# RWKV mixer, heads 6 to 11: half of the matrices with exchanged chunk partitions, common units for all heads, a new order

## Chip, cores and metric

One core of a Trainium2 chip runs the whole kernel in one launch. The metric is the device time of one execution in microseconds (us); the time before is the median of three runs, 1074.89 us (1074.24 to 1075.43). The profile is of one execution more, 1075.53 us, whose span from first to last instruction is 1073.7 us.

## What is computed

A trunk of two layers on 256 tokens of width 1024, batch 1, all in float32. Each layer is a SwiGLU feed-forward (width 2816), a mixer with memory attention beside it, and a second SwiGLU, each followed by a layer norm. Layer 0's mixer is RWKV-7 with 12 heads of 64, layer 1's a stick-breaking attention.

```
for i in range(2):
    x = LN(ALPHA*x + 0.5*swiglu(x, ffn1[i]))
    p = x @ W_in[i]
    mix = rwkv7(p) if i == 0 else stick_breaking(p)
    h = concat(mix, memory_attention(p))
    x = LN(ALPHA*x + h @ w_out[i])
    x = LN(ALPHA*x + 0.5*swiglu(x, ffn2[i]))
# RWKV-7, for each head and token:
sa    = state @ kk_t
state = state*w_t - outer(sa, kk_t*a_t) + outer(v_t, k_t)
out_t = state @ r_t        # then a norm over the head, a bonus r.k.r_k * v, and a gate
```

## The kernel before

**Tiling.** The 256 tokens are two halves of 128, one token a partition. A feed-forward is 11 blocks of 256 columns. A block loads its gate, up and down weights (3 MB, six or more pieces of 128x1024), splits each piece into a high and a low part (`hi` on ScalarE, `lo` on VectorE; `piece`, line 638), and multiplies by three fp32r matmuls for each product (`mm3`, line 666). In a "whole" block the down weights stay plain f32 and take one f32 matmul instead. A block can be run for both halves on one load, or for one half ("solo", line 1503), so that one half's feed-forward can fill TensorE while the other half is in its mixer.

**The RWKV mixer** (`rwkv`, line 968) works on one half, which has two chunks of 64 tokens. A chunk's recurrence becomes triangular 64x64 matrices a head: `L` and its inverse (`T`, and its transpose `Tt`, built from 16x16 blocks by two rounds of products with `Lm` and `Y`), `Sk` and `RB` (decayed key and receptance products), `V`, and the turned `kn` and `bn`. In these tiles partitions 0 to 63 hold chunk 0 and partitions 64 to 127 chunk 1, for all 12 heads. Two heads share a state tile `S` by partitions. The last part is, chunk by chunk: X = Sk V (+ q S), U = -Tt X, S = S + kn V + bn U, output = Sk' V + r S + RB U.

Every one of these products is 64 rows by 64 columns. The partitions of its operands fix the row group of TensorE that it uses, the partitions of its result the column group. `product` (line 1233) multiplies six heads for both chunks, with operands and result on the same partitions; the loops of lines 1275 to 1339 do the rest.

**Order.** No instruction is issued as it is written: `Plan` (line 134) records all of them with an estimated cost, `order` (line 349) makes a list schedule for the five engines, and `improve` (line 545) repeats that `ROUNDS` times from a random seed and keeps the order that its own estimate finds shortest. Instructions in a `together` block (line 147) stay one unit on TensorE. `alternate` (line 1477) runs a mixer and feed-forward blocks of the other half side by side: each `yield` of the mixer adds the weight that the table `RW` has for its name, and for each 1.0 one step of filler follows. `LAGS`, `FIRST`, `HOLD` and `TAIL` say which blocks are solo and where they stand; `NRAW`, `NHI`, `NLO` are the buffers of weight pieces; `copy` (line 212) may go to ScalarE or VectorE. PSUM has two banks of each of four names: `gu`, `tp`, `acc0`, `acc1`.

Since all instructions are issued from line 602, the profile names groups by tiles: `T_339r`, `Y_340r` and so on are buffers, and later tiles in the same buffer carry the first one's name: X stands in `L_345r` (L), U and the transposed b in `Lm_330r`, V in `vn_311r`, kn in `kn_310r`, bn in `bn_384r`.

Of the kernel before, what the change touches and what calls it, by code (L numbers as in the profile page):

```python
# [21 lines left out]
P = 128  # L22
# [5 lines left out]
C = 64  # L28
# [35 lines left out]
MEMTAG = 'gu'  # L64
# [3 lines left out]
ORDERS = ((0, 1, 2, 3), (3, 0, 1, 2), (1, 0, 3, 2), (3, 0, 1, 2))  # L68
# [58 lines left out]
ROUNDS = 24  # L127
SHAKES = (0.0, 100.0, 300.0)
PATIENCE = 8
SEED = 8617  # L130
# [475 lines left out]
def kernel(ctx, tc, const, x, mem, f1g, f1u, f1d, f2g, f2u, f2d, ln_g, ln_b, w_out, w_mem_kv,  # L606
# [361 lines left out]
    def rwkv(hf, res):  # L968
# [54 lines left out]
        gate = sl("g")  # L1023
        for g in range(2):
            gp = ps(ac)
            nc.tensor.matmul(gp[:, :384], zl[:, 1], R["gup"][:, g * 384:(g + 1) * 384], start=True, stop=True)
            nc.copy(gate[:, g * 384:(g + 1) * 384], gp[:, :384])
# [73 lines left out]
        def nat(src, dst):  # L1101
            for j0, n in ((0, 4), (4, 2)):
                pt = ps("tp")
                with nc.together():
                    for i in range(n):
                        nc.tensor.transpose(pt[:, i * P:(i + 1) * P], src[:, j0 + i], ident)
                nc.copy(dst[:, j0 * P:(j0 + n) * P], pt[:, :n * P])

        hv = lambda t: t.rearrange("p (h d) -> p h d", d=HD)
        par = lambda t: t.rearrange("q (j p) d -> q j p d", p=2)  # L1110
        v = zv.rearrange("p j t -> p (j t)")
        nat(zv, v)
        V = hv(v)

# [10 lines left out]
        def narrow(a, b):  # L1125

            banks = [ps(next(tg))[:, :384].rearrange("q (j t) -> q j t", j=NT) for _ in range(2)]
            with nc.together():
                for j in range(NT):
                    for p, c in ((0, 0), (1, 1), (1, 0), (0, 1)):  # L1130
                        pr, cs = slice(p * HD, (p + 1) * HD), slice(c * C, (c + 1) * C)
                        nc.tensor.matmul(banks[p][cs, j], a(pr, j, cs), b(pr, j, cs), start=True, stop=True)
            yield from enumerate(banks)
# [54 lines left out]
        def put_back(x, scratch, dst):  # L1188
            nc.vector.transpose(scratch, x)
            sv = v4(scratch, True)[:, :, :, :NH]  # L1190
            for b in range(2):
                src = sv[:, :, b].rearrange("p s h -> p h s")
                nc.copy(dst[:, :, BLK * b:BLK * b + BLK], src, quad[:, 0:1])
                nc.copy(dst[:, :, 32 + BLK * b:32 + BLK * b + BLK], src, quad[:, 1:2])

        for p, sv in narrow(lambda *i: bt[i], lambda *i: qr[i[0], i[1], 1, i[2]]):
            nc.vector.tensor_tensor(par(RB)[:, :, p], sv, bc(mqr[:, 1], 1, [P, NT, C]), ALU.mult)
            yield "rb"
        for g in range(2):
            js = slice(3 * g, 3 * g + 3)  # L1200
            banks = [ps(next(tg))[:, :384].rearrange("q (i x t) -> q i x t", i=3, x=2) for _ in range(2)]
            with nc.together():
                for i in range(3):
                    for p, c in ((0, 0), (1, 1), (1, 0), (0, 1)):
                        pr, cs = slice(p * HD, (p + 1) * HD), slice(c * C, (c + 1) * C)
                        nc.tensor.matmul(banks[p][cs, i], kt[pr, 3 * g + i, cs], qr[pr, 3 * g + i, :, cs], start=True, stop=True)
# [9 lines left out]
        put_back(Xs[0], sl("Tt")[:, :512], T)  # L1216
        s2 = sl("Y")[:, :512]
        Tt = hv(sl("Tt"))
        put_back(Xs[1], s2, Tt)

        Lm = hv(sl("Lm"))
        for lastl in (False, True):
# [10 lines left out]
            def product(a, b, g, tag):  # L1233
                sv = ps(tag)[:, :384].rearrange("q (i t) -> q i t", i=6)
                with nc.together():
                    for i in range(6):
                        for c in range(2):
                            cs = slice(c * C, (c + 1) * C)
                            nc.tensor.matmul(sv[cs, i], a[cs, 6 * g + i], b[cs, 6 * g + i], start=True, stop=True)
                return sv  # L1240

            for g in range(2):
                gs = slice(6 * g, 6 * g + 6)
                tag = (ac, "tp")[g]
                y = product(Lm, Tt, g, tag)
                nc.copy(Y[:, gs], y)
                yield "dy"
            for g in range(2):
                gs = slice(6 * g, 6 * g + 6)
                tag = (ac, "tp")[g]  # L1250
                if not lastl:
                    tn = product(Y, T, g, tag)
                    yield "dt"
                ttn = product(T, Y, g, tag)
                yield "dt"
                if not lastl:
                    nc.vector.tensor_sub(T[:, gs], T[:, gs], tn)
                nc.vector.tensor_sub(Tt[:, gs], Tt[:, gs], ttn)

        hb = hv(sl("T"))  # L1260
        nc.vector.tensor_tensor(hb, V, bc(vm, 2, [P, NH, HD]), ALU.add)
        nc.vector.tensor_tensor(hb, hb, bc(bon, 2, [P, NH, HD]), ALU.mult)
# [3 lines left out]
        nc.vector.tensor_tensor(lb, lb, hv(gate), ALU.mult)  # L1266
        lg = hv(sl("T"))
        nc.sync.dma_start(lg, r_lng[0].partition_broadcast(P).rearrange("p (h d) -> p h d", d=HD))
        nc.vector.tensor_tensor(lg, lg, hv(gate), ALU.mult)

        X, U, o = hv(sl("L")), hv(sl("Lm")), hv(sl("Y"))
        six = lambda tag: [ps(tag)[:, :384].rearrange("q (i t) -> q i t", i=6) for _ in range(2)]
        both = [slice(c * C, (c + 1) * C) for c in range(2)]
        xb, Ov = six("tp"), six(ac)
        with nc.together():
            for i in range(NH):
                for cs in both:
                    nc.tensor.matmul(xb[i // 6][cs, i % 6], Sk[cs, i, 0], V[cs, i], start=i % 6 == 0, stop=i % 6 == 5)
        nc.copy(X[:, 0:6], xb[0])
        nc.copy(X[:, 6:12], xb[1])  # L1280
        yield "c0"
        own = []

        def from_pairs():
            with nc.together() as made:
                for i in range(NH):
                    for c, cs in enumerate(both):
                        nc.tensor.matmul(Ov[i % 2][cs, i // 2], Sk[cs, i, 1], V[cs, i], start=i < 2 and (hf == 0 or c == 1), stop=False)
            own.extend(made)

        if hf == 0:
            from_pairs()
        for c, cs in enumerate(both):
            first = hf == 0 and c == 0
            before = []
            if not first:
                with nc.together() as before:
                    for j in range(NT):
                        for p in range(2):
                            pr = slice(p * HD, (p + 1) * HD)  # L1300
                            nc.tensor.matmul(Ov[p][cs, j], qr[pr, j, 1, cs], S[pr, j], start=j == 0 and c == 0, stop=False)
                xs = six("tp")
                with nc.together() as made:
                    for j in range(NT):
                        for p in range(2):
                            pr = slice(p * HD, (p + 1) * HD)
                            nc.tensor.matmul(xs[p][cs, j], qr[pr, j, 0, cs], S[pr, j], start=True, stop=True)
                made[0].after.append(before[0].i)
# [3 lines left out]
            ub = six("tp")  # L1312
            with nc.together() as made:
                for i in range(NH):
                    nc.tensor.matmul(ub[i // 6][cs, i % 6], Tt[cs, i], X[cs, i], start=True, stop=True)
                    if c == 1:
                        nc.tensor.matmul(Ov[i % 2][both[0], i // 2], RB[both[0], i], U[both[0], i], start=False, stop=i >= NH - 2)
            solved = made[0].i
            if hf > 0 and c == 0:
                from_pairs()  # L1320
                own[0].after.append(solved)
            nc.copy(U[cs, 0:6], ub[0][cs], -1.0)
            nc.copy(U[cs, 6:12], ub[1][cs], -1.0)
            yield "c2"
            if not (hf == NHALF - 1 and c == 1):
                sb = ps("tp")[:, :MIX // 2].rearrange("q (j d) -> q j d", j=NT)
                for a, b in ((kn, V), (bn, U)):
                    with nc.together() as made:
                        for h in range(NH):
                            pr = slice(h % 2 * HD, (h % 2 + 1) * HD)  # L1330
                            nc.tensor.matmul(sb[pr, h // 2], a[cs, h * HD:(h + 1) * HD], b[cs, h],
                                             start=a is kn and h < 2, stop=a is bn and h >= NH - 2)
                made[0].after.append(own[0].i)
                nc.vector.tensor_tensor(S, S, sb, ALU.add)
                nc.vector.tensor_tensor(S, S, bc(pc[:, :, c], 2, [P, NT, HD]), ALU.mult)
                yield "c3"
        with nc.together():
            for i in range(NH):
# [234 lines left out]
```

## Time and profile before

| | us | share of the span |
|---|---|---|
| median of three runs | 1074.89 | |
| the profiled execution | 1075.53 | |
| its span | 1073.7 | |
| TensorE (PE) busy | 1055.9 | 98% |
| VectorE (DVE) busy | 880.6 | 82% |
| ScalarE (ACT) busy | 730.2 | 68% |
| weight queue, 302.12 MB | | 85% of 16 DMA engines |

PE is TensorE's matmuls, PEld its weight loads. Matmuls overlap: the length given for one is longer than the distance to the next, so the pace of a unit is read from starts. An f32 matmul leaves two records, an fp32r matmul one. "x24" is the number of records merged in a row. In the view of waits a row is: who waited <- for whom: total us, times, longest.

### The profile page before, as it was taken

The numbers are of one execution on the slowest core, as the hardware profiler recorded it, in microseconds if no ns is written. First come the engines' busy times: TensorE is split into PE (matmuls) and PEld (weight loads), VectorE is DVE, ScalarE is ACT, GpSimd is POOL, SyncE is SP. The second block draws the span as 40 slices with busy tenths as digits, with TensorE's granted clock in tenths as the row PEclk, the third lists the DMA queues.
The fourth block names the chain that finished last, engine by engine and source line by source line (L and its number), as shares of the span: only waits on it lengthen the run. The fifth ranks groups of instructions, "written<-read, shape, count | busy, mean of one in ns | idle before, by whom it ended". The sixth has DMA issues, their size and how long they took to land.

```text
span 1073.7 us, 17563 instructions
## 1 busy us (share of the span) xinstructions
PE 1055.9 (98%) x6253; PEld 848.2 (79%) x6253; DVE 880.6 (82%) x1227; ACT 730.2 (68%) x1037; POOL 4.3 (0%) x18
## 2 busy tenths in 40 slices
PE   7999999999999999999999999999999999999996
PEld 5888887877778777778888888888777777888885
DVE  5676669897999997886699865659799989998796
ACT  5665558865689784565577655538896999767672
POOL 0000000000000000000000000000000000000000
PEclk9999999999999999999999999999999999999999
DMA  9997869677888797698989976658988988999892
GB/s 292 334 364 250 255 207 357 203 241 240 257 292 290 243 303 252 204 345 293 296 290 365 342 231 205 216 174 293 366 268 293 366 294 281 371 367 347 292 328 90
DMA packets 212538, 303.24 MB, mean 282 GB/s; under 512 B 13876, under 2 KB 159456, under 8 KB 212450
## 3 DMA queue, kind: packets, MB, share of 16 engines
q1 hardware_dynamic: 212450, 302.12, 85.0%
q8 instruction: 49, 0.80, 0.3%
q14 instruction: 39, 0.32, 0.1%
HBM read 301.01 MB, written 1.05 MB: 281 GB/s over the span
## 4 chain that ended last, share of the span: by engine, by line
PE 94%; DVE 4%; DMA 1%; ACT 1%; issue 0%; SPq 0%; DVEq 0%; ACTq 0%
PE ps_26r L602 29%; PE ps_27r L602 28%; PE ps_24r L602 8%; PE ps_25r L602 8%; PE ps_22r L602 7%; PE ps_23r L602 7%; PE ps_2r L602 4%; PE ps_3r L602 4%; DVE x L602 1%; DMA raw_12r<-in_sb_w_in_dram 1%; DMA raw_6r<-in_ffn_w_up_dram 0%; DVE lo_5r L602 0%; DVE st_564r L602 0%; DVE Y_340r L602 0%; DVE lo_44r L602 0%
## 5 line engine op out<-in xcount | busy, mean ns | idle before, releaser
L602 ACT ACTIVATE h_31r<-ps_27r 128x256 f32<-128x256 f32 (+1 forms) x43 | 17.7, 411 | 29.4 <-PE ps_27r L602 29.0
L602 ACT ACTIVATE h_32r<-ps_26r 128x256 f32<-128x256 f32 (+1 forms) x41 | 17.6, 429 | 20.7 <-PE ps_26r L602 20.7
L602 PE MATMUL ps_26r<-hi_4r,xTh 128*128 128x512 f32 (+1 forms) x66 | 27.0, 409 | 1.9 <-ACT hi_4r L602 1.9
L602 PE MATMUL ps_26r<-lo_5r,xTh 128*128 128x512 f32 (+1 forms) x66 | 26.0, 394 | 0.5 <-DVE lo_5r L602 0.5
L602 PE MATMUL ps_26r<-hi_4r,xTl 128*128 128x512 f32 (+1 forms) x66 | 25.9, 392 | 0.0
L602 PE MATMUL ps_27r<-hi_16r,xTh 128*128 128x512 f32 x54 | 22.4, 414 | 0.0
L602 PE MATMUL ps_27r<-hi_7r,xTh 128*128 128x512 f32 x52 | 22.2, 427 | 0.0
L602 PE MATMUL ps_26r<-hi_13r,xTh 128*128 128x512 f32 x50 | 21.0, 419 | 1.2 <-ACT xTh L602 1.2
L602 PE MATMUL ps_26r<-hi_19r,xTh 128*128 128x512 f32 (+1 forms) x54 | 22.0, 407 | 0.0
L602 PE MATMUL ps_26r<-hi_7r,xTh 128*128 128x512 f32 x52 | 21.7, 417 | 0.0
L602 PE MATMUL ps_27r<-hi_13r,xTh 128*128 128x512 f32 x52 | 21.6, 415 | 0.0
L602 PE MATMUL ps_27r<-hi_16r,xTl 128*128 128x512 f32 x54 | 21.2, 392 | 0.0
L602 PE MATMUL ps_27r<-lo_17r,xTh 128*128 128x512 f32 x54 | 21.1, 390 | 0.0
L602 PE MATMUL ps_26r<-hi_7r,xTl 128*128 128x512 f32 x52 | 20.8, 400 | 0.0
L602 PE MATMUL ps_26r<-lo_8r,xTh 128*128 128x512 f32 x52 | 20.8, 400 | 0.0
L602 PE MATMUL ps_27r<-hi_10r,xTh 128*128 128x512 f32 x50 | 20.7, 415 | 0.0
L602 PE MATMUL ps_26r<-hi_19r,xTl 128*128 128x512 f32 (+1 forms) x54 | 20.7, 383 | 0.0
L602 PE MATMUL ps_26r<-lo_20r,xTh 128*128 128x512 f32 (+1 forms) x54 | 20.6, 382 | 0.0
L602 PE MATMUL ps_27r<-hi_13r,xTl 128*128 128x512 f32 x52 | 20.4, 392 | 0.0
L602 PE MATMUL ps_27r<-hi_7r,xTl 128*128 128x512 f32 x52 | 20.3, 391 | 0.0
L602 PE MATMUL ps_27r<-lo_8r,xTh 128*128 128x512 f32 x52 | 20.3, 390 | 0.0
L602 PE MATMUL ps_27r<-lo_14r,xTh 128*128 128x512 f32 x52 | 20.3, 390 | 0.0
(1873 smaller groups left out, 3948.0 us busy)
## 6 DMA issues: line engine op xcount, KB each, us to landing
raw_39r<-in_ffn_w_down_dram SPq DMA_DIRECT2D x17, 512.0 KB, 6.1
raw_12r<-in_ffn_w_gate_dram SPq DMA_DIRECT2D x32, 256.0 KB, 5.6
raw_12r<-in_ffn_w_up_dram SPq DMA_DIRECT2D x32, 256.0 KB, 6.7
raw_18r<-in_ffn_w_down_dram SPq DMA_DIRECT2D x16, 512.0 KB, 5.9
raw_42r<-in_ffn_w_down_dram SPq DMA_DIRECT2D x16, 512.0 KB, 5.5
raw_21r<-in_ffn_w_down_dram SPq DMA_DIRECT2D x15, 512.0 KB, 5.9
raw_48r<-in_ffn_w_gate_dram SPq DMA_DIRECT2D x30, 256.0 KB, 5.5
raw_48r<-in_ffn_w_up_dram SPq DMA_DIRECT2D x30, 256.0 KB, 6.8
```

What stands on the lines that cost most here:

```text
L602: fn(*[at(x) for x in a], **{n: at(x) for n, x in k.items()})
```

## The change

Heads 6 to 11 (group g = 1) keep half of their matrices with the chunks exchanged: chunk 1 on partitions 0 to 63, chunk 0 on 64 to 127. Exchanged are V, kn, bn, Sk, RB, T, Y and U; not exchanged are L, Lm, Tt and X. A product of an exchanged matrix with another then reads one partition half and writes the other, and `products` interleaves both groups in one unit.

```diff
+        def put(dst, pt, g):
+            at = slice(384 * g, 384 * g + 384)
+            for to, ts in ((slice(0, P), slice(0, P)),) if g == 0 else (chunk, chunk[::-1]):
+                nc.copy(dst[to, at], pt[ts])
...
+        hb = hv(sl("g"))
+        for g in range(2):
+            pt = three(zv, g)
+            gs = slice(6 * g, 6 * g + 6)
+            nc.vector.tensor_tensor(hb[:, gs], hv(pt), bc(bon[:, gs], 2, [P, 6, HD]), ALU.mult)
+            put(v, pt, g)
...
+        def products(banks, a, b, crossed, turned_out, cs=(0, 1), start=True, stop=True):
+            for i in range(6):
+                for g in range(2):
+                    for c in cs:
+                        rows, to = chunk[c ^ (g & crossed)], chunk[c ^ (g & turned_out)]
+                        h = 6 * g + i
+                        nc.tensor.matmul(banks[g][to, i], a[rows, h], b[rows, h], start=start and i == 0, stop=stop and i == 5)
+            return banks
...
-            for g in range(2):
-                y = product(Lm, Tt, g, tag)
-                nc.copy(Y[:, gs], y)
+            with nc.together():
+                y = products(six((ac, "tp")), Lm, Tt, 0, 1)
+            for g in range(2):
+                nc.copy(Y[:, 6 * g:6 * g + 6], y[g])
...
+                    n = products(six((ac, "tp")), T if x else Y, Y if x else T, 1, 1 - x)
...
+            xb = products(six("tp"), Sk[:, :, 0], V, 1, 0)
...
+            products(Ov, Sk[:, :, 1], V, 1, 0, stop=False)
...
+                            for x in range(2):
+                                nc.tensor.matmul(xs[p][chunk[c ^ x], j], qr[pr, j, x, cs], S[pr, j], start=j == 0, stop=j == NT - 1)
...
+                for p in range(2):
+                    nc.copy(par(o)[cs, :, p], xs[p][chunk[1 - c]])
...
+                ub = products(six("tp"), Tt, X, 0, 1, (c,))
...
+                                    h, rows = 6 * g + 2 * i + p, chunk[c ^ g]
+                                    nc.tensor.matmul(sb[g][p * HD:(p + 1) * HD, i], a[rows, h * HD:(h + 1) * HD], b[rows, h],
+                                                     start=a is kn and i == 0, stop=a is bn and i == 2)
...
+            products(Ov, RB, U, 1, 0, start=False)
```

The part r S of the output no longer accumulates in the output's bank: it is written to the other column group of X's bank, copied to the tile `o`, and the rest is added to it at the end. `put_back` writes T in twelve copies instead of four. The products for RB and Sk (`narrow` and the loop after it) write heads 6 to 11 to the exchanged partitions. The gate's product moves from the start of the mixer to behind the inverse, and the bonus is multiplied from PSUM as soon as V is there.

The order's numbers change with it:

```diff
-NRAW = 10
+NRAW = 11
-NLO = 9
+NLO = 8
-LAGS = ((5, 8), (4, 9))
-FIRST = 2
+LAGS = ((5, 9), (4, 9))
+FIRST = 4
-RW = dict(p0=0, p1=0, p2=0, p3=0, p4=0.5, lb=0, sub=14, rb=0.5, kq=1, nat=10, dy=4, dt=1.5, c0=8, c1=3, c2=6, c3=2, t0=0, t1=1.5)
+RW = dict(p0=0, p1=0, p2=0, p3=0, p4=0.5, lb=0, sub=14, rb=0.5, kq=1, nat=10, dy=4, dt=1, c0=8, c1=3, c2=12, c3=1.5, t0=1.5, t1=1.5)
-HOLD = (2, 3)
+HOLD = (1, 4)
-BOOST = 18.0075
-TANH = (((0, 1, 2, 3, 4), (0, 1, 2, 3, 5, 9)), ((0, 1, 2, 3, 9), (0, 1, 2)))
-WHOLE = (((1, 2, 3, 4, 5, 6, 8, 9), (0, 1, 2, 4, 5, 6, 7, 9)), ((3,), ()))
+BOOST = 16.0075
+TANH = (((0, 1, 2, 3, 4, 5), (1, 2, 3, 5, 9)), ((0, 1, 2, 3, 8, 9), (0, 1, 2)))
+WHOLE = (((1, 2, 3, 4, 5, 6, 8, 9), (0, 1, 2, 4, 5, 6, 7)), ((3,), (6,)))
-MEMTAG = 'gu'
+MEMTAG = 'acc1'
-ORDERS = ((0, 1, 2, 3), (3, 0, 1, 2), (1, 0, 3, 2), (3, 0, 1, 2))
+ORDERS = ((3, 1, 2, 0), (1, 0, 2, 3), (1, 0, 3, 2), (3, 0, 1, 2))
-ROUNDS = 24
+ROUNDS = 185
-SEED = 8617
+SEED = 1031
```

More of the change, by code (lines that the diff above doesn't have):

```diff
@@ L1123, in rwkv, with narrow @@
         tg = iter([ac, "tp"] * 40)
-        def narrow(a, b):
+        def narrow(a, b, crossed=False):
             banks = [ps(next(tg))[:, :384].rearrange("q (j t) -> q j t", j=NT) for _ in range(2)]
@@ L1260, in rwkv @@
-        hb = hv(sl("T"))
-        nc.vector.tensor_tensor(hb, V, bc(vm, 2, [P, NH, HD]), ALU.add)
-        nc.vector.tensor_tensor(hb, hb, bc(bon, 2, [P, NH, HD]), ALU.mult)
+            with nc.together():
+                y = products(six((ac, "tp")), Lm, Tt, 0, 1)
+            yield "dy"
+            for g in range(2):
+                nc.copy(Y[:, 6 * g:6 * g + 6], y[g])
+                yield "dy"
+            for x in (0, 1) if not lastl else (1,):
+                with nc.together():
+                    n = products(six((ac, "tp")), T if x else Y, Y if x else T, 1, 1 - x)
+                yield "dt"
+                for g in range(2):
+                    gs = slice(6 * g, 6 * g + 6)
+                    if x:
+                        nc.vector.tensor_sub(Tt[:, gs], Tt[:, gs], n[g])
+                    else:
+                        keep = n
+                yield "dt"
+                if x and not lastl:
+                    for g in range(2):
+                        gs = slice(6 * g, 6 * g + 6)
+                        nc.vector.tensor_sub(T[:, gs], T[:, gs], keep[g])
@@ L1263, in rwkv @@
+        gate = hv(sl("T"))
+        for g in range(2):
+            gp = ps(ac)
+            nc.tensor.matmul(gp[:, :384], zl[:, 1], R["gup"][:, g * 384:(g + 1) * 384], start=True, stop=True)
+            nc.copy(gate[:, 6 * g:6 * g + 6], hv(gp[:, :384]))
         lb = hv(sl("lb"))
@@ L1265, in rwkv @@
         nc.vector.tensor_tensor(lb, lb, hb, ALU.add)
-        nc.vector.tensor_tensor(lb, lb, hv(gate), ALU.mult)
-        lg = hv(sl("T"))
+        nc.vector.tensor_tensor(lb, lb, gate, ALU.mult)
+        lg = hv(sl("g"))
         nc.sync.dma_start(lg, r_lng[0].partition_broadcast(P).rearrange("p (h d) -> p h d", d=HD))
-        nc.vector.tensor_tensor(lg, lg, hv(gate), ALU.mult)
+        nc.vector.tensor_tensor(lg, lg, gate, ALU.mult)
         X, U, o = hv(sl("L")), hv(sl("Lm")), hv(sl("Y"))
-        six = lambda tag: [ps(tag)[:, :384].rearrange("q (i t) -> q i t", i=6) for _ in range(2)]
-        both = [slice(c * C, (c + 1) * C) for c in range(2)]
-        xb, Ov = six("tp"), six(ac)
+        if hf == 0:
+            nc.gpsimd.memset(o[chunk[0]], 0.0)
         with nc.together():
[L1276 to L1280, printed above, removed]
-        yield "c0"
[L1282 to L1297, printed above, removed]
+            xb = products(six("tp"), Sk[:, :, 0], V, 1, 0)
+        Ov = six(ac)
+        for g in range(2):
+            nc.copy(X[:, 6 * g:6 * g + 6], xb[g])
+        yield "c0"
+        with nc.together():
+            products(Ov, Sk[:, :, 1], V, 1, 0, stop=False)
+        for c, cs in enumerate(chunk):
+            if hf > 0 or c > 0:
+                xs = six("tp")
+                with nc.together():
                     for j in range(NT):
@@ L1300, in rwkv @@
                             pr = slice(p * HD, (p + 1) * HD)
[L1301 to L1307, printed above, removed]
@@ L1313, in rwkv @@
[L1313 to L1322, printed above, removed]
@@ L1323, in rwkv @@
-            nc.copy(U[cs, 6:12], ub[1][cs], -1.0)
+            with nc.together():
+                ub = products(six("tp"), Tt, X, 0, 1, (c,))
+            for g in range(2):
+                to = chunk[c ^ g]
+                nc.copy(U[to, 6 * g:6 * g + 6], ub[g][to], -1.0)
             yield "c2"
             if not (hf == NHALF - 1 and c == 1):
-                sb = ps("tp")[:, :MIX // 2].rearrange("q (j d) -> q j d", j=NT)
+                sb = six("tp", 3)
                 for a, b in ((kn, V), (bn, U)):
[L1328 to L1334, printed above, removed]
+                    with nc.together():
+                        for i in range(3):
+                            for g in range(2):
+                                for p in range(2):
+                                    h, rows = 6 * g + 2 * i + p, chunk[c ^ g]
+                                    nc.tensor.matmul(sb[g][p * HD:(p + 1) * HD, i], a[rows, h * HD:(h + 1) * HD], b[rows, h],
+                                                     start=a is kn and i == 0, stop=a is bn and i == 2)
+                for g in range(2):
+                    nc.vector.tensor_tensor(S[:, 3 * g:3 * g + 3], S[:, 3 * g:3 * g + 3], sb[g], ALU.add)
```

85 lines of the change are left out of this document (33 added, 52 removed).

## The prediction

> **What bounds the kernel now.** I read the page's totals first, then the waits of TensorE, then the busy time by stage, and only then single instructions.
>
> ```profile
> span 1073.7 us, 17563 instructions
> PE 1055.9 (98%) x6253; PEld 848.2 (79%) x6253; DVE 880.6 (82%) x1227; ACT 730.2 (68%) x1037; POOL 4.3 (0%) x18
> PEclk9999999999999999999999999999999999999999
> PE 94%; DVE 4%; DMA 1%; ACT 1%; issue 0%; SPq 0%; DVEq 0%; ACTq 0%
> ```
>
> TensorE (PE) is busy 98% of the span at full clock, and 94% of the chain that ended last is PE. A busy PE can still hide waits, so next what PE waited for:
>
> ```profile
> PE ps_2r L602 <- DMA x<-in_x_dram: 4.6, 1, 4.6
> PE ps_26r L602 <- ACT hi_4r L602: 1.9, 1, 1.9
> PE ps_26r L602 <- ACT xTh L602: 1.2, 1, 1.2
> PE ps_2r L602 <- ACT memKT L602: 0.6, 1, 0.6
> PE ps_26r L602 <- DVE lo_5r L602: 0.5, 1, 0.5
> ```
>
> The waits sum to 8.8 us, and 4.6 + 1.9 + 0.5 of that is the start. Between the RWKV stages and the end nearly nothing is left to save by waiting less; time is saved by giving PE less to do. The stage in which the change sits, and one stretch for comparison, as busy time by window (columns: window, its length, busy PE, PEld, DVE, ACT, POOL, clock, DMA share, GB/s):
>
> ```profile
> 160.00:300.00 140.00, 139.29 (x1329) 110.22 (x1329) 126.27 (x215) 102.80 (x186) 1.84 (x6) 1.00 0.79 261
> 300.00:320.00 20.00, 20.00 (x96) 16.29 (x95) 19.59 (x33) 16.53 (x24) 0.00 (x0) 1.00 0.82 279
> 320.00:440.00 120.00, 120.00 (x1218) 91.91 (x1217) 105.65 (x185) 86.01 (x152) 1.21 (x3) 1.00 0.80 263
> 900.00:960.00 60.00, 60.00 (x274) 49.44 (x273) 58.00 (x72) 45.98 (x54) 0.00 (x0) 1.00 1.04 358
> ```
>
> Both RWKV halves run between 160 and 440 us, with feed-forward blocks as filler. PE has no idle time there; VectorE (DVE) is the next engine, 251.5 of 280 us, 90%.
>
> **The change: narrow products.** A 64x64 product uses one of four quadrants of PE: its row group is the partitions it reads, its column group those it writes. How fast a unit goes depends on how many quadrants its neighbours in the queue can use. Each f32 matmul leaves two records: the kn*V unit has 12 matmuls in the code and 24 records below. Two quadrants, from the order of PE's instructions (start, length, what, records):
>
> ```profile
> 245.71 0.87 PE L602 MATMUL ps_22r<-Y_340r,T_339r 64*64 64x64 f32 x24
> 246.41 0.87 PE L602 MATMUL ps_2r<-T_339r,Y_340r 64*64 64x64 f32 x24
> 247.10 0.87 PE L602 MATMUL ps_3r<-Y_340r,T_339r 64*64 64x64 f32 x24
> ```
>
> Start to start is 0.70 us for 12 matmuls, two at a time: 6 rounds of 0.117 us. One quadrant (Tt*X, 12 matmuls), and one row group with both column groups (kn*V, bn*U):
>
> ```profile
> 261.31 0.91 PE L602 MATMUL ps_2r<-L_345r,Tt_329r 64*64 64x64 f32 x12
> 262.06 0.86 PE L602 MATMUL ps_3r<-L_345r,Tt_329r 64*64 64x64 f32 x12
> 262.85 1.12 PE L602 MATMUL ps_24r<-raw_18r,hT_486r 128*128 128x512 f32 x2
> 263.91 0.92 PE L602 MATMUL ps_2r<-vn_311r,kn_310r 64*64 64x64 f32 x24
> 264.65 0.87 PE L602 MATMUL ps_2r<-Lm_330r,bn_384r 64*64 64x64 f32 x24
> ```
>
> Tt*X takes 1.54 us, which is 12 rounds (1.40) and 0.14 of entering and draining; kn*V takes 0.74, 6 rounds, although both its quadrants share a row group. All four quadrants are in use already in the units that were built head by head from the transposed side:
>
> ```profile
> L602 PE MATMUL ps_3r<-Lm_330r,qr_377r 64*64 64x64 f32 x48 | 1.8, 222 | 0.0
> ```
>
> ```profile
> 213.46 0.27 PE L602 MATMUL ps_22r<-Lm_330r,qr_377r 64*64 64x64 f32 x1
> ...
> 214.21 0.28 PE L602 MATMUL ps_23r<-qr_377r,Lm_330r 64*64 64x64 f32 x2
> ```
>
> The x48 of bank ps_3r are two halves, 24 each, and the unit fills two banks: 24 matmuls in 0.75 us. So a round costs 0.117 us whether it holds one matmul, two or four, and I count rounds.
>
> The Trainium skill, TensorE: Matmul & The Clock Gate, under The mechanism, has weight loads overlap matmuls in flight only where the row group differs; by it the new Tt*X, whose two quadrants share one, would stay at 12 rounds, 2.8 us less would be saved, and the forecast would be 1062.3, still inside its own range. The kn*V row disagrees: 6 rounds from one row group.
>
> Per half, before and after, from the code:
> - Lm*Tt, twice: 12 rounds to 6 each, 12 saved. T*Y (the one that makes Tt), twice: 12 saved. Y*T: its rows and columns are both exchanged, so both head groups meet in the same two quadrants: nothing.
> - Sk*V for X and for the output: 12 to 6 each, 12 saved.
> - Tt*X and RB*U: before 12 (chunk 0), 12 (chunk 1, with RB*U of chunk 0 beside it), 12 (RB*U of chunk 1); after 6 + 6 + 6: 18 saved.
>
> That is 54 a half, 108 in all. The state products qr*S, run three times (not for the first chunk): 12 to 6, 18 saved. kn*V and bn*U, three times: together 12 to 6, 18 saved. Sum 144 rounds, **16.8 us** of PE.
>
> **What it adds on PE.** Block 6 of the second feed-forward in layer 1 becomes "whole" (plain f32) for half 0. From the chain in order of time (start, length, tile, matmul records):
>
> ```profile
> 441.86 4.08 PE ps_24r L602 x18
> 453.42 0.86 PE ps_22r L602 x2
> ```
>
> A split product is three records of 0.227, 0.68 us; a plain one 0.86. Four of them: +0.7 us. The other lists change only entries beyond their loops or the table functions. LAGS 8 to 9 moves half 0's block 8 beside the RWKV stage: PE's sum is the same, since it multiplies each half by itself anyway.
>
> Each visit of PE to the 64x64 mode costs something of its own:
>
> ```profile
> 415.74 0.39 PE L602 MATMUL ps_27r<-hi_7r,xTl 128*128 128x512 f32 x1
> 416.06 0.91 PE L602 MATMUL ps_3r<-L_345r,Tt_329r 64*64 64x64 f32 x12
> ...
> 276.41 0.50 PE L602 MATMUL ps_27r<-hi_7r,hi_13r 128*128 128x512 f32 x1
> 276.75 0.39 PE L602 MATMUL ps_27r<-lo_8r,hi_13r 128*128 128x512 f32 x1
> ```
>
> The last wide matmul ahead takes 0.32 instead of 0.23, the first one behind 0.34, with the 0.14 above 0.34 us in all. Common units cannot be fewer visits than the chain has links; I count 26 visits now and estimate three more, since units that used to stand back to back now wait for both copies: +1.0 us (bounds: five fewer, -1.7; eight more, +2.7).
>
> **What lies beside PE.** A common unit needs both head groups' inputs, so a gap opens at each link:
>
> ```profile
> 244.06 0.49 ACT L602 ACTIVATE Y_340r<-ps_22r 128x384 f32<-128x384 f32 x1 [0.53 <-PE ps_22r L602]
> 244.70 0.49 ACT L602 ACTIVATE Y_340r<-ps_2r 128x384 f32<-128x384 f32 x1
> 244.96 0.91 PE L602 MATMUL ps_23r<-T_339r,Y_340r 64*64 64x64 f32 x24
> ```
>
> Today T*Y starts on the first copy while the second runs. After, two copies of 0.49 and the hand-overs on either side stand between Lm*Tt and T*Y, about 1.3 us, with the filler's 0.7 us plain matmul or wide matmuls to cover it. Behind the waiting unit on PE's queue stand whichever filler matmuls the order put there; if they are put ahead of it, nothing is lost. I take 0 of it (the waits above show fillers covering every such gap now) and keep the other end for a rival.
>
> ```profile
> L602 DVE TENSOR_TENSOR lo_44r<-raw_12r,hi_43r 128x1024 fp32r<-128x1024 f32 x11 | 13.4, 1221 | 4.7 <-ACT hi_43r L602 4.7
> L602 ACT ACTIVATE L_345r<-ps_3r 128x384 f32<-128x384 f32 x4 | 2.0, 488 | 1.5 <-PE ps_3r L602 1.3 <-DVE T_339r L602 0.2
> q1 hardware_dynamic: 212450, 302.12, 85.0%
> ```
>
> ScalarE (ACT): exchanged partitions split copies. Three turned matrices a half (+0.5 us each), the T blocks (twelve small copies for four) and the state output (+1.0, three times) make about +11 us by the 0.49 us row, in an engine with 75 us free in that stage. DVE: the bonus reads PSUM once instead of two passes over 768, the tail multiplies once more; it cancels. Block 8 loaded apart for each half adds six splits, 7.3 us of DVE, about as much ACT, and 3.1 MB over 302, 1% of the queue. All this hides while PE is the bound; if DVE becomes it, the second rival applies. SP's queue gets ten more weight loads (eight of gate and up, two of down) and one more buffer (NRAW 11) to run ahead. The later gate product is the same matmul at another place: nothing.
>
> **Sum.** 1075.5 (profiled execution, 1073.7 of it the span) - 16.8 + 0.7 + 1.0 = 1060.4. The median of the runs lies 0.6 below the profiled one, so 1059.8; the 1.2 and 0.6 us waits on xTh and memKT sit at places the new order rearranges, between 0 and -1.8, and I take -0.3: **1059.5 us**.
>
> **Rivals.**
> 1. *A bank takes one row group at a time.* In the new units both row groups feed each bank, except in qr*S, kn*V, bn*U and Tt*X. Then only those would gain: 18 + 18 + 24 rounds, 7.0 us, and the time is 1069.3. Against it: ps_22r alone took 12 matmuls from both row groups in 0.70 us. The Trainium skill, TensorEngine Tiling, under Gotcha 1: PSUM Pressure, says "Different row tiles cannot access same PSUM bank simultaneously". The trace differs, at two row groups in one bank; four quadrants on two such banks it does not show. Chance 5%.
> 2. *DVE becomes the bound of 160 to 440.* There PE falls to 280 - 16.8 + 1.0 + 8.2 (block 8, 36 x 0.227) = 272.4, DVE rises to 251.5 + 7.3 + 0.8 = 259.6: 95%. If DVE packs only to 92.5%, the stage takes 280.7 and the kernel 1068. For it: DVE holds PE's operands and the RWKV chain in one queue, and NLO falls to 8. Against it: in 900 to 960 DVE runs at 97% beside a PE without idle time. Chance 13%.
> 3. *The gaps of the common units stay open: slower.* Ten links a half, 20 in all, each up to 1.3 us without filler: +26, about 1085. It ends above the present time from 0.77 us uncovered a link (15.4 over 20). Against it: two plain or four wide matmuls fill a link, and the half-1 stage has one block more of them than before. Chance 4%.
> 4. *More than the work is saved*: fewer visits and no wait behind the start: 1055.5. Chance 4%.
>
> **How the numbers follow.** The forecast holds 74%: 1056 to 1063, made of the visits (-2.7 to +1.7 about my value), 0 to -1.8 of waits and some 2 us of uncovered gaps. The range reaches into rival 2 and to the edge of rival 4: 1055 to 1067. This kernel can be told from no change at about 0.2%, 2.1 us. Faster: 74 + 13 + 5 + 4 less 1 for a DVE that packs no better than today's 90% (289 us of stage, about 1076) = 95%; that 1% is "same"; slower 4%.
>
> **What would show it.** Right: the new T*Y, Sk*V and RB*U units hold 24 matmuls in 0.70 to 0.75 us and kn*V some 0.35; the 64x64 share of PE falls by about 16 us; PE stays at 98%. Rival 1: those units take 1.40. Rival 2: PE waits on lo tiles between 160 and 440 us. Rival 3: PE waits on Y, X, U or Tt. Wrong altogether would be a PE share below 97%, or a changed wait for weights in the longer runs of blocks for one half (FIRST 4 after TAIL 3), where the DMA queue works at its most (358 GB/s in 900 to 960) and has little left.

## The result, and the profile after

The changed kernel takes **1067.13 us** (median of 4 runs, 1066.09 to 1068.49), the kernel before 1074.9 us in the same comparison: ratio 0.9929, 95% interval 0.9912 to 0.9946. It is faster by 7.8 us, half of the 15.4 us that were forecast, and lies 0.13 us above the forecast's range. The profiled execution took 1068.49 us, the longest of the four. Page totals and PE's waits after:

```profile
span 1066.7 us, 17867 instructions
PE 1044.2 (98%) x6249; PEld 832.7 (78%) x6249; DVE 884.1 (83%) x1238; ACT 752.3 (71%) x1068; POOL 5.1 (0%) x19
PEclk9999999999899999999999999999999999999999
```

```profile
PE ps_3r L602 <- DVE hs_561r L602: 4.2, 1, 4.2
PE ps_2r L602 <- DMA x<-in_x_dram: 4.1, 1, 4.1
PE ps_26r L602 <- ACT hi_4r L602: 2.9, 1, 2.9
PE ps_23r L602 <- DVE mv_567r L602: 0.7, 1, 0.7
PE ps_2r L602 <- ACT h_32r L602: 0.6, 1, 0.6
```

The share of busy time is 98% as before and would tell nothing. The new row is the first one: PE stood still once, for 4.2 us, and slice 11 of the clock shows an 8. The windows around that place (length, busy PE, PEld, DVE, ACT, POOL, then the clock, DMA share, GB/s), and the two RWKV stages as before:

```profile
160.00:300.00 140.00, 134.78 (x1328) 103.94 (x1327) 127.47 (x222) 106.32 (x196) 2.58 (x7) 0.98 0.78 262
280.00:284.00 4.00, 0.12 (x1) 0.12 (x2) 3.90 (x19) 1.87 (x6) 0.00 (x0) 1.00 0.38 115
284.00:288.00 4.00, 3.39 (x20) 2.62 (x22) 4.00 (x13) 2.81 (x6) 0.00 (x0) 0.58 0.07 6
288.00:292.00 4.00, 4.00 (x24) 3.49 (x21) 3.54 (x7) 1.58 (x3) 0.00 (x0) 0.57 0.51 142
300.00:440.00 140.00, 140.00 (x1343) 105.51 (x1342) 127.82 (x219) 118.33 (x198) 1.21 (x3) 1.00 0.84 281
```

From 240 to 300 us PE is idle for 5.2 us (0.7 before), and behind the hole it runs at 0.57 of its clock: 3.39 x 0.42 + 4.00 x 0.43 = 3.1 us more. Half 1's stage from 300 to 440 us has no idle time at all.

Did the products shrink? The new units, in the order of PE's instructions (Sk*V, RB*U, kn*V, bn*U, first matmuls only):

```profile
277.39 0.27 PE L602 MATMUL ps_23r<-vn_311r,Sk_341r 64*64 64x64 f32 x2
...
278.14 0.23 PE L602 MATMUL ps_23r<-Lm_330r,RB_333r 64*64 64x64 f32 x2
...
278.84 0.22 PE L602 MATMUL ps_3r<-vn_311r,kn_310r 64*64 64x64 f32 x1
...
279.19 0.22 PE L602 MATMUL ps_3r<-Lm_330r,bn_381r 64*64 64x64 f32 x1
```

24 matmuls take 0.75 and 0.70 us, kn*V 0.35, as forecast. Added over all 1440 records of 64x64, from each start to the next matmul's start and without the hole, they cost 44.3 us before and 28.1 after: 16.2 us saved.

A stage's length can be read from the statistics of the layer norms (`BATCH_NORM_STATS2` on DVE): behind the feed-forward of half 0, behind half 0's `mixed_out`, behind half 1's. `mixed_out` has two column blocks with one record each, and the first one counts. Before, then after:

```profile
149.59 1.28 DVE L602 BATCH_NORM_STATS2 st_283r<-x 128x6 f32<-128x512 f32 x2
...
301.32 0.69 DVE L602 BATCH_NORM_STATS2 st_283r<-x 128x6 f32<-128x512 f32 x1
...
446.69 0.69 DVE L602 BATCH_NORM_STATS2 st_564r<-x 128x6 f32<-128x512 f32 x1
```

```profile
149.22 1.28 DVE L602 BATCH_NORM_STATS2 st_283r<-x 128x6 f32<-128x512 f32 x2
...
299.27 0.69 DVE L602 BATCH_NORM_STATS2 st_283r<-x 128x6 f32<-128x512 f32 x1
...
446.76 0.69 DVE L602 BATCH_NORM_STATS2 st_566r<-x 128x6 f32<-128x512 f32 x1
```

Half 0's stage went from 151.73 to 150.05 us, although its 64x64 products cost 7.9 us less and 8 fp32r matmuls (1.8 us) left it. Half 1's went from 145.4 to 147.5 us, with 8.2 us less of 64x64 and some 9 us of filler more (27 fp32r, 8 plain records). **Half 1 kept its gain but for about 1 us, half 0 gave 8.0 us back** (9.7 expected from the products and the fillers, 1.7 seen): 4.5 us of added idle time and 3.1 of clock make 7.6 of them. Both kernels reach the end of half 1's stage at 446.7 us; the time gained lies behind it, because the filler that moved into half 1's stage is missing there. These are single executions: in another one of the same order (`reduce3_1`, below) half 0's stage took 148.6 us, by which 6.6 us would have been given back.

### The profile page after: what moved, and what is told of

Same layout as the page of the kernel before. It is cut to its first block, busy times and chain, and to the rows that moved or that the text cites. A ratio compares the mean times of both kernels' runs of the same rounds, so it can differ in the third digit from the quotient of the medians.

```text
span 1066.7 us, 17867 instructions
## 1 busy us (share of the span) xinstructions
PE 1044.2 (98%) x6249; PEld 832.7 (78%) x6249; DVE 884.1 (83%) x1238; ACT 752.3 (71%) x1068; POOL 5.1 (0%) x19
## 4 chain that ended last, share of the span: by engine, by line
PE 97%; DVE 1%; DMA 0%; ACT 0%; SPq 0%; issue 0%; DVEq 0%; ACTq 0%
PE ps_27r L602 29%; PE ps_26r L602 29%; PE ps_25r L602 8%; PE ps_24r L602 8%; PE ps_22r L602 8%; PE ps_23r L602 8%; PE ps_3r L602 4%; PE ps_2r L602 3%; DMA raw_6r<-in_ffn_w_up_dram 0%; DVE x L602 0%; DVE st_566r L602 0%; SPq L602 0%; DVE mv_567r L602 0%; DVE hs_561r L602 0%; DVE lo_5r L602 0%
## 5 line engine op out<-in xcount | busy, mean ns | idle before, releaser
L602 ACT ACTIVATE h_31r<-ps_26r 128x256 f32<-128x256 f32 (+1 forms) x56 | 23.2, 414 | 28.2 <-PE ps_26r L602 27.5
L602 ACT ACTIVATE h_32r<-ps_27r 128x256 f32<-128x256 f32 (+1 forms) x54 | 23.3, 431 | 24.6 <-PE ps_27r L602 24.5
L602 PE MATMUL ps_27r<-lo_38r,xTh 128*128 128x512 f32 x74 | 28.9, 390 | 0.0
L602 PE MATMUL ps_27r<-lo_14r,xTh 128*128 128x512 f32 x72 | 28.1, 390 | 0.0
L602 PE MATMUL ps_26r<-lo_38r,xTh 128*128 128x512 f32 (+1 forms) x68 | 26.1, 384 | 0.0
L602 PE MATMUL ps_26r<-lo_11r,xTh 128*128 128x512 f32 x64 | 25.0, 390 | 0.0
L602 PE MATMUL ps_27r<-hi_40r,xTh 128*128 128x512 f32 x60 | 24.3, 406 | 0.0
L602 PE MATMUL ps_27r<-lo_5r,xTh 128*128 128x512 f32 x62 | 24.2, 390 | 0.0
L602 PE MATMUL ps_27r<-hi_40r,xTl 128*128 128x512 f32 x60 | 23.5, 391 | 0.0
L602 PE MATMUL ps_27r<-hi_19r,xTh 128*128 128x512 f32 x54 | 22.0, 407 | 0.0
L602 PE MATMUL ps_27r<-lo_11r,xTh 128*128 128x512 f32 x56 | 21.9, 390 | 0.0
```

The costliest lines, as they stand in the source:

```text
L602: fn(*[at(x) for x in a], **{n: at(x) for n, x in k.items()})
```

## The experiments

Stage lengths below are read in the same way, one profiled execution each; idle is 60 us less PE's busy time in the window 240 to 300. The same order can differ by 1.5 us in half 0's stage from one execution to another (150.1 and 148.6 us, the changed kernel and `reduce3_1`). Where the order differs, a stage also holds more or less filler (in `memory_first` and `held` half 0's has 20 fp32r matmuls, some 4.6 us, more than in the changed kernel), so those lengths are compared with care and the medians decide. `short0` leaves out half 0's gate factor and the exchange of T, `bare0` and `bare0_last` leave out the low part of the weights in four blocks; the other runs do the whole computation.

| run | median us | ratio to before, 95% | half 0 | half 1 | idle 240-300 |
|---|---|---|---|---|---|
| before | 1074.9 | | 151.7 | 145.4 | 0.7 |
| changed | 1067.13 | 0.9929 (0.9912-0.9946) | 150.1 | 147.5 | 5.2 |
| products_only | 1080.99 | 1.0056 (1.0043-1.0070) | 153.1 | 152.2 | 6.6 |
| order_only | 1084.26 | 1.0084 (1.0070-1.0098) | 158.1 | 154.4 | 4.0 |
| dve_first | 1068.72 | 0.9942 (0.9929-0.9956) | 149.8 | 147.7 | 4.4 |
| warm | 1066.20 | 0.9919 (0.9906-0.9933) | 148.5 | 147.5 | 2.5 + 3.5 of dummies |
| memory_first | 1069.58 | 0.9954 (0.9939-0.9969) | 152.4 | 146.8 | 2.7 |
| memory_first_warm | 1069.34 | 0.9951 (0.9936-0.9966) | 151.0 | 146.8 | 0.8 + 3.4 |
| reduce3_0 | 1068.87 | 0.9951 (0.9936-0.9965) | 150.8 | 147.4 | 6.7 |
| reduce3_1 | 1068.31 | 0.9946 (0.9929-0.9963) | 148.6 | 149.2 | 4.6 |
| twice0 | 1077.11 | 1.0024 (1.0014-1.0033) | 157.0 | 147.0 | 6.1 |
| twice1 | 1076.00 | 1.0016 (1.0007-1.0026) | 149.7 | 155.8 | 4.5 |
| short0 | 1071.03 | 0.9968 (0.9954-0.9982) | 151.0 | 149.9 | 5.2 |
| bare0 | 1069.32 | 0.9954 (0.9939-0.9968) | 150.4 | 151.1 | 6.3 |
| held | 1071.95 | 0.9975 (0.9966-0.9985) | 157.0 | 145.4 | 7.5 |
| numbers | 1068.17 | 0.9939 (0.9926-0.9953) | 149.9 | 147.4 | 5.1 |
| bare0_last | 1064.48 | 0.9905 (0.9888-0.9921) | 146.9 | 146.1 | 2.9 |
| last | 1069.80 | 0.9960 (0.9945-0.9975) | 151.2 | 148.6 | 5.4 |

### Code and numbers apart

`products_only` has the changed code and the numbers of before (only `ROUNDS` is 185); `order_only` is the reverse.

> The code of the changed kernel (exchanged partitions, common units) with the numbers of the kernel before (buffers, lags, due times, lists, bank of the memory products, seed); only the number of rounds of improvement of the order is that of the changed one. Theory A (the products are worth their 16 us only where other work stands ready, so what is kept depends on the order): a part of the gain is lost, 1067 to 1074, and the lost part stands as PE waits between 240 and 300 us. Rival D (the products alone bring the forecast, and the new numbers cost 8 us): 1058 to 1061.

> The code of the kernel before with the numbers of the changed one. Theory A: no gain from the numbers alone, 1073 to 1078, and half 0's stage without a hole of 4 us, since the old products keep PE busy. Rival D (the new numbers cost about 8 us whatever the products): 1081 to 1084, with the hole in it.

Each alone is slower than before, by 6.2 and 9.5 us; together they are 7.8 us faster. `order_only` came out 0.3 us above where rival D put it, but then `products_only` should have taken 1060 and took 1081, beyond theory A as well: neither part has a price of its own. The numbers were chosen for one code, and a code with other durations seems to need others. In `products_only` PE is idle in both stages (6.6 us from 240 to 300, 3.7 from 300 to 440). So the same 16 us less of PE work brought a gain with one set of numbers and none with another. `order_only` shows one thing more: with the old products, too, PE is idle for 4.0 us at half 0's end, in pieces of at most 1.5 us, and the clock falls to half for 10 us. The shorter products alone therefore cannot be blamed for the idle time there; the new numbers open it as well.

### The hole and the clock

```diff
# dve_first: DVE's place of four operations of half 0's end
+MOVED = ((1252, 1124), (1149, 1124), (1148, 1124), (1260, 1158))   # operation, ahead of which
# warm: behind the last bn*U (1147) four f32 matmuls 128x512 into an unused bank
+EXTRA = {1147: 4}
```

> The changed kernel with the same order on every engine, except that on DVE the reciprocals of half 0's memory softmax and the two additions to the state S stand ahead of half 0's output tail instead of behind it. Theory A (in half 0 the chain decides, not PE's work: after the last bn*U PE has nothing ready, and stands 4.2 us because DVE reaches these four operations 3.5 us late): the hole at 280 us shrinks from 4.2 to between 1 and 2.5 us, and the time falls by 2 to 4 us from 1067.1, to 1063 to 1065. Rival B (the hole only shows that the products for it were used up, and the output tail on DVE, which now ends about 0.9 us later, decides when PE can go on): the hole moves behind the transposes, and the time stays within 1 us of 1067.1.

> The changed kernel with the same order, and four plain f32 matmuls 128x512 more (0.86 us each, 3.4 us of PE), into an unused PSUM bank, directly behind the last bn*U of half 0, in the hole of 4.2 us; nothing reads them. Theory A (PE is not the bound there): the time does not rise by 3.4 us. Theory C (the idle stretch also costs by the lower clock of the 7 to 8 us behind it: 0.57 to 0.58 granted): the transposes behind it take 0.11 us each instead of 0.21, the granted clock of 284 to 292 is above 0.9, and the time falls by 1 to 3 us. If the low clock lies beside DVE's tail anyway: the clock is up and the time within 0.7 us of 1067.1. Rival (PE is the bound there too): +3.4 us.

In `dve_first` the wait fell apart, and nothing was won (1068.72 us, 0.6 above what rival B allowed):

```profile
PE ps_3r L607 <- DVE g_424r L607: 1.9, 1, 1.9
PE ps_3r L607 <- DVE hs_561r L607: 1.6, 1, 1.6
PE ps_2r L607 <- ACT h_32r L607: 0.8, 1, 0.8
```

1.9 + 1.6 + 0.8 is 4.3: a part of the hole moved behind the first transposes, where PE waited for x (the 1.6), as rival B said. `warm` kept the clock at 1.00 throughout and absorbed 3.5 us of useless PE work without getting slower (0.9 us below the changed kernel, with overlapping intervals). So PE is not the bound there, and the low clock costs at most a microsecond or two; the output tail on DVE, which runs beside it, would explain that. The hole ends here, in the changed kernel, on PE, on ACT and on DVE:

```profile
283.88 0.84 PE L602 MATMUL ps_3r<-cst,h_31r 128*128 128x128 f32 x4 [4.17 <-DVE hs_561r L602]
```

```profile
283.32 0.91 ACT L602 ACTIVATE h_31r<-h_31r,rs_599r 128x256 f32<-128x256 f32 x2 [2.13 <-DVE mv_567r L602]
```

```profile
280.93 0.95 DVE L602 TENSOR_REDUCE hs_561r<-L_342r 128x12 f32<-128x768 f32 x1
...
283.07 0.16 DVE L602 RECIPROCAL rs_599r<-rs_599r 128x2 f32<-128x2 f32 x1
...
283.20 0.35 DVE L602 TENSOR_TENSOR S_110r<-S_110r,ps_3r 128x192 f32<-128x192 f32 x1
...
288.59 0.56 DVE L602 TENSOR_TENSOR Y_337r<-Y_337r,lb_433r 128x384 f32<-128x384 f32 x1
```

Two chains meet: the memory's softmax and the RWKV output (`hs`, `Y`), both through DVE's queue, and `mixed_out` needs both. PE's row names `hs`, but what it turns is `h_31r`, and ACT could only scale that behind the reciprocal `rs`, which stands behind `hs` in DVE's queue. `memory_first` therefore exchanged some 60 places behind the last bn*U on all engines, and `memory_first_warm` adds dummies:

> The changed kernel with the same instructions, in another order for some 60 of them behind the last bn*U of half 0: on DVE the state additions and the softmax reciprocals first and norm(1)'s last two passes behind the output tail; on PE the four products of mixed_out that read only the memory's output (2.7 us) ahead of the transposes of x and of the RWKV output. Theory A (half 0's end is a chain on DVE, 10 us long behind the last bn*U, with too little on PE's queue that is ready): real work fills a part of the hole, the first product on the RWKV output no longer waits behind them, and the time falls by 2 to 4 us, to 1063 to 1065. Rival B (DVE is full from 277 to 290, so that an exchange in its queue only moves the hole, as it did with the state additions alone): 1066.5 to 1069. The granted clock may still fall behind the first wait.

> The same as the other order with the memory's products first, and four plain f32 matmuls 128x512 (3.4 us, read by nothing) in the waits behind bn*U and behind the two transposes of the softmax. Theory A with the clock: the granted clock stays at 1.0 through 278 to 292 and the time is 0.7 to 2 us below the run without them. Without an effect of the clock: the same within 0.5 us. If PE is the bound there: up to 3.4 us above it.

With the dummies the hole was gone (0.8 us idle), and both medians were still above the changed kernel's (by 2.5 and 2.2 us, 0.6 above rival B's range in the first case). The wait came back at 308 us, where PE has done the next projections and needs the x that comes out of half 0's `mixed_out`:

```profile
310.73 0.66 PE L611 MATMUL ps_3r<-cst,x 128*128 128x128 f32 x4 [2.26 <-DVE x L611]
```

So the wait moved, as rival B says. The kept clock made no difference (1069.58 and 1069.34).

### Does an operation in the tail count?

```diff
# reduce3_0, reduce3_1: the reduction hs is issued three times in one half's tail
+AGAINS = {1157: 3}     # reduce3_1: {2031: 3}
-                for fn, a, k in o.calls:
+                for fn, a, k in o.calls * AGAINS.get(o.i, 1):
```

> The changed kernel with the same order; the reduction hs over 128x768 on DVE in half 0's output tail is done three times (the same result each time): 1.9 us more on DVE, nothing more on PE. Theory A (half 0's end waits for this chain on DVE): the whole 1.9 us shows, 1068.5 to 1069.5, with the hole of PE at 6 us. Rival B' (PE is the bound, the hole is an accident of the order): under 0.7 us.

> The same threefold reduction in half 1's output tail (at some 435 us) instead of half 0's. Theory A (half 1 has products in store, PE is the bound there, and this is why half 1 kept all of its 8 us): 0, within 0.5 us of the changed kernel. If the chain decides in half 1 as well: +1.9 us.

```profile
PE ps_3r L603 <- DVE hs_561r L603: 6.1, 1, 6.1
```

```profile
PE ps_3r L603 <- DVE Y_337r L603: 1.5, 1, 1.5
```

In half 0 the hole grew from 4.2 to 6.1 us, the whole 1.9. In half 1, in the second row, PE waited 1.5 us where it had not waited at all, and the stage grew by 1.7; the median rose by 1.2. **This was expected to be zero.** Here a stage without idle time on PE had no slack in its chain either. Both runs keep the changed kernel's order; what a new order would have absorbed is not shown.

### Is the PE time worth its length?

```diff
-            for i in range(6):
+            for i in [*range(6)] * (2 if hf == H and start and stop and not (crossed and turned_out) else 1):
# twice0: H = 0, SEED 8617; twice1: H = 1; ROUNDS 60 in both, planned anew
```

> The changed kernel with the new units Lm*Tt, T*Y (the one for Tt), Sk*V for X and Tt*X issued twice over in half 0 alone (same result): 42 rounds, 4.9 us of PE, are given back there; the order is planned anew from the true costs, so 1 to 2 us of difference belong to the order. Theory A (half 0's end is decided by serial chains, so the PE time saved there was not kept): up to 2 us above the changed kernel, 1067 to 1069.5. Rival E (the products were worth their PE time in half 0 as well, and the longer chain of the rest of the change, its copies and its tail, took it back): the full 4.9 us, 1071 to 1073.

> The same doubling of 42 rounds in half 1 alone, planned anew. Both theories: PE is full there and the trace of the changed kernel shows the whole 8 us kept, so 4.9 us more, 1071 to 1073. If it costs less than 2 us, PE does not decide in half 1 either, and the reading of the stages is wrong.

Half 0's stage grew by 7.0 us over the changed kernel's, half 1's by 8.3, for 4.9 us of PE each, and the other half stayed. Both medians are above the range of 1071 to 1073, by 4.1 and 3.0 us. By their records the 64x64 products took 7.3 us more in half 0, where 3.3 us of their time fell into 10 us of half clock, and 5.4 us more in half 1, which also got 2.3 us of idle time. Theory A falls: PE's time in half 0 was not free (the unit lies on the chain and on PE). So the products' saving should have counted in both halves, and something else in half 0 took it back; how much of the rise is the new order's, these two runs can't tell.

### What took it back?

```diff
# short0
-        put_back(Xs[0], sl("Tt")[:, :512], T, True)
+        put_back(Xs[0], sl("Tt")[:, :512], T, hf != 0)
+        if hf != 0:      # both passes over 128x768: lg * gate, o * lg
# bare0: four blocks of half 1's feed-forward beside half 0's RWKV
-            made.append(nc.vector.tensor_sub(lo, raw, hi.bitcast(F32)))
+            if low: ...
```

> The changed kernel with a shorter chain in half 0: T is copied back without exchanging partitions (4 copies instead of 12), and the gate's gain lg (two passes over 128x768 on DVE) is left out, so half 0's RWKV output is another one; some 5 us less of chain on ACT and DVE, no PE work less; planned anew. Theory A (the RWKV chain alone ends half 0): the hole closes, 1062 to 1064. Rival F (a second chain, memory products - softmax - transposes, ends at the same time): the hole stays, 1065 to 1069.

> The changed kernel with 16 of DVE's splits (128x1024, 1.14 us each by their spacing, 18 us of DVE) left out in half 0's stage: four blocks of the feed-forward of half 1 multiply by the rounded weights twice instead of by the rest, so their result is less exact; PE's work is the same; planned anew. Rival G (DVE's throughput bounds half 0's stage, 97% busy from 200 to 240, as the second rival of the prediction had it): 1061 to 1064. Theory A and F (latency of chains, not throughput): the hole stays, 1065 to 1070.

Neither closed the hole (5.2 and 6.3 us idle; 1071.03 us, above both ranges, and 1069.32 us), although the last RWKV product, counted from the stage's start, came 2.7 and 6.3 us earlier than in the changed kernel. The trace of `bare0` says why; DVE and then PE:

```profile
278.89 1.02 DVE L603 TENSOR_TENSOR Y_337r<-Y_337r,lb_433r 128x384 f32<-128x384 f32 x2
```

```profile
286.62 0.95 PE L603 MATMUL ps_3r<-cst,h_31r 128*128 128x128 f32 x4 [2.69 <-ACT h_32r L603]
...
291.18 0.50 PE L603 MATMUL ps_22r<-hi_7r,xTh 128*128 128x512 f32 x1 [0.47 <-ACT xTh L603]
```

The RWKV output was complete at 279.9 us, 9 us earlier than in the changed kernel, and the first product of `mixed_out` still began at 291.2 (290.8 in the changed kernel): `ORDERS` puts the memory's block first, and the softmax was late. One run put the cover back where before had it, the other changed the order's numbers alone:

```diff
# held
+                    if 2 * k + hf >= 2 * KT - 9:      # memory_kv's last nine products
+                        nc.ops[-1].after.append(B["held"])   # behind RB*U of half 0
# held also ORDERS[0] = (0, 1, 2, 3), WAIT 16.8, HOLD (1, 5), SEED 2; numbers: WAIT 16.8, ORDERS[0] = (3, 2, 0, 1); ROUNDS 45 in both
```

> The changed kernel with a cover for half 0's tail: the last nine split products of memory_kv (6.1 us of PE) may only start behind RB*U of half 0, as they stood in the kernel before by the order alone, and the memory's part of mixed_out comes last instead of first, so that the softmax chain lies beside the products on the RWKV output; planned anew (with other values of two waiting numbers and the seed). Theory H (the missing cover at this one place is what cost the 8 us, 4.2 to 5.5 of wait and the low clock behind it): no wait above 1 us behind 275 us, clock at 1.0, and 1060 to 1064. Rival I (PE's work in half 0's stage is simply shorter than its chain, and who covers the tail is missing at the links): waits of 0.5 to 1.6 us between 255 and 275, 4 to 6 us in all, and 1064 to 1068.

> The changed kernel with three other numbers of its order: WAIT 16.8 for 10.76, the order of mixed_out's blocks in half 0 3-2-0-1 for 3-1-2-0, fewer rounds. The same products, the same chains. Theory I: half 0's waits are spread into pieces of 0.4 to 1.7 us instead of one of 4.2 and are as long in sum; what may be won is the clock, 0 to 3 us: 1064 to 1067. If the hole is an accident of the numbers: 1059 to 1062.

`held` was worse (1071.95 us, above both ranges): without those fillers PE waited between the product units, and its clock fell for ten microseconds:

```profile
260.00:270.00 10.00, 8.06 (x250) 5.81 (x250) 6.76 (x10) 3.80 (x7) 0.73 (x1) 1.00 0.91 333
270.00:280.00 10.00, 5.91 (x144) 5.32 (x144) 2.64 (x6) 2.76 (x6) 0.64 (x3) 0.50 0.02 5
```

`numbers` spread the idle time (5.1 us, pieces of at most 1.4, clock 1.00) and gained nothing either (1068.17 us, 1.2 above theory I's range). In both places of the cover, 5 us or more are missing. The last two runs eased both chains, or only the memory's:

```diff
# last: ORDERS[0] = (1, 0, 2, 3), ROUNDS 60; bare0_last: the same on bare0, SEED 1
```

> As the run without 16 of DVE's splits in half 0's stage (four blocks multiply by the rounded weights instead of the rest, so the result is less exact; 18 us less of DVE, PE's work the same), and mixed_out of half 0 takes its blocks in the order 1-0-2-3, the memory's last, instead of 3-1-2-0, the memory's first; another seed, planned anew. In the run with the memory's block first the RWKV output lay ready at 279.9 us, 9 us earlier than in the changed kernel, and mixed_out still began at 291 because its first block waited for the softmax. Theory J (two chains end half 0, the RWKV chain held up by DVE's queue and the memory's softmax, and each alone keeps the hole open): with both out of the way the wait shrinks to below 2 us in one piece and the time falls by 4 to 8 us, to 1059 to 1063. If a third thing holds the stage (weights, buffers): 1066 to 1070.

> The changed kernel with only the order of half 0's blocks in mixed_out changed to 1-0-2-3 (the memory's last); planned anew. Theory J: the RWKV chain, which ends at 289 us, still holds mixed_out, so the time does not fall: 1067 to 1072. If the order of these blocks alone was the error: 1060 to 1064.

`last` alone lost 2.7 us against the changed kernel. Together with the 18 us less of DVE the idle time fell to 2.9 us, no wait behind the start was above 0.7, the clock stayed at 1.00, and half 0's stage took 146.9 us, 3.2 less than changed. The time, 1064.5, is above the 1059 to 1063 expected and 2.7 us below the changed kernel, with intervals that just overlap; the run also has a seed of its own. 2.9 us of idle pieces remain, and their cause was not tried.

None of the runs with the full computation beats the changed kernel by more than the uncertainty; `warm` is the lowest, at 1066.20.

## Why the prediction was half right

**Held.** PE's rounds: 24 matmuls in 0.70 to 0.75 us, kn*V 0.35, Tt*X with one row group and both column groups 0.84, 12 rounds in a row (1.40 us) left only in Y*T. The sum was -16.8 and +1.0 for three more visits of PE to the 64x64 mode; measured -16.2, with exactly three visits more (26 to 29). Rival 1 (one row group a bank) is refuted by the units themselves. The whole block (12 fp32r records fewer, 8 plain ones more) and the start behaved as costed, within a microsecond: the start's three waits rose from 7.0 to 7.5.

**Failed: "I take 0 of it (the waits above show fillers covering every such gap now)" and "All this hides while PE is the bound".** Both steps priced longer links of the chain at nothing, because the cover was there before the change. The links were covered, as the first one says: from the first Lm*Tt to the last bn*U PE is idle for only 0.45 us. What had no price was the cover itself. In that stretch PE now does 17.8 us of other work (fillers, and 1.6 us of the gate's product) instead of 13.9, while half 0's stage has less of it to give, so it is missing behind the last product. There the second step fails: PE stands 4.2 us, and `warm` and `reduce3_0` show that DVE's chain and not PE is the bound. ACT itself rose by 22 us where some 18 were forecast. T's copies are one of the longer links, ACT after:

```profile
240.46 1.89 ACT L602 ACTIVATE T_336r<-Tt_329r,cst 128x96 f32<-128x96 f32 x4 [0.28 <-DVE Tt_329r L602]
...
248.16 1.14 ACT L602 ACTIVATE Tt_329r<-Y_337r,cst 128x192 f32<-128x192 f32 x2
```

From the transposed T on DVE to the last copy of Tt it is now 240.4 to 249.3, 8.9 us, with two splits of weight pieces (2.1 us on ACT) among the copies; before, four and four copies ended 4.4 us behind it. I had counted ACT's free 75 us, not its place on the chain. The first Lm*Tt began at 249.7 instead of 243.0 us; from there to the last bn*U it takes 29.8 us instead of 33.2, so 8 us less of PE shortened the chain by 3.4. The last product ends 3.2 us later than before, while the fillers that used to cover the tail (eleven split products from 276.4 to 284.0 us) are done by 271.1. The last matmul of these fillers, before and after:

```profile
283.81 0.39 PE L602 MATMUL ps_27r<-hi_4r,lo_41r 128*128 128x512 f32 x1
```

```profile
270.80 0.40 PE L602 MATMUL ps_27r<-hi_4r,lo_11r 128*128 128x512 f32 x1
```

**What is shown and what is not.** Shown: behind half 0's last product PE is not the bound (`warm` took in 3.5 us of useless work, `reduce3_0` made PE wait 1.9 us longer for 1.9 us more on DVE); PE's time in either half is not free (`twice0`, `twice1`); PE there waits now for the softmax, now for the RWKV output, and easing one of them made the kernel no faster (`short0`, `bare0`, `last`). Argued only: that the two chains together hold the 8 us (`bare0_last`, which eased both, won 2.7 us, but with a new order and overlapping intervals); that the shorter products opened the hole (the new numbers do so with the old products too, in `order_only`); and how the longer chain of half 0 divides among the split copies, the wait of both groups for each other and the order of DVE's queue. Every change of code also changes the order, and runs of one code with other numbers differ by 1 to 14 us (`numbers`, `products_only`). Half 1 had 9 us more of filler, which may be why it kept its gain; a run that gives half 0 as much was not made.

**Rivals.** Rival 2 (DVE becomes the bound, 1068, 13%) gave the right time by luck: its sign, PE waiting on `lo` tiles between 160 and 440 us, is not among the waits, and DVE was hardly fuller (127.5 of 140 us, 126.3 before). What counted in `reduce3_0` was DVE's queue at half 0's end, not its load over the stage. Rival 3 named waits on Y, X, U or Tt at the links, and none is there; the gap opened at the end, behind the last link: 5.2 us in place of up to 26. "PE stays at 98%" was a poor test, since it held.

## What to carry to other kernels

Where PE is always busy only because other work was put beside serial chains to cover them, saving PE time also removes cover: stage by stage, subtract from the gain what the chain, with its new links, is longer than the work left. A copy, an extra pass or a wait for a second operand is free only if the cover still exists after the change; where the order was packed by a search, don't count on slack (here 1.9 us on DVE added 1.5 to 1.9 us to PE's waits in either half, with the order kept). Code and order have to be judged together: each alone made this kernel slower.

## What the hardware showed

- The granted clock fell after short waits too. In `dve_first` PE stood still for 1.93 us, and of the next two microseconds the clock was 0.66 and 0.50; in the changed kernel, after 4.17 us, it fell at about 285 us, behind the end of the wait, and came back at 291. In `numbers`, with waits up to 1.4 us, it stayed at 1.00, and in `twice0` it fell at 286.1 us although no single wait in the 20 us before it was above 0.74 us (PE was busy for 2.2 of the 3 us from 283); so the length of one wait does not decide alone. The Trainium skill, TensorE: Matmul & The Clock Gate, under HAM oscillation, gives about 3.4 us as the idle gap from which the clock falls; `dve_first` differs, at 1.93 us.
- A clock at half for 7 us cost little where PE was not the bound: half 0's stage took 148.5 us with the clock kept up (`warm`) and 148.6 and 150.1 us without (`reduce3_1`, the changed kernel).
- Four quadrants into two banks, each fed by both row groups, keep the pace of 0.117 us a round. The Trainium skill, TensorEngine Tiling, under Gotcha 1: PSUM Pressure, would forbid this at once for two row tiles in one bank; 24 matmuls in 0.70 us disagree.
